# Layer 2 of a two-layer decoder trunk: weight splits of the gate's first units one step ahead, and the order of the splits at the start of the output projection

## The chip, the core and the metric

The kernel runs on one core of a Trainium2 chip. The metric is the device time of one execution in microseconds (us); lower is better. TensorE (PE in the profile, PEld for its weight loads) does the matrix products, VectorE (DVE) and ScalarE (ACT) do the elementwise work, GpSimd (POOL) takes a few small operations and issues the stores, and SyncE (SP) issues nearly all loads. Each engine takes its instructions strictly in the order in which the program lists them; between engines they wait for semaphores.

## The reference

Two layers of a decoder trunk, 512 tokens, width 2048, all in float32. The parts that matter here belong to layer 2, multi-head latent attention:

```
mod = (c_act @ ada_w[i] + ada_b[i])[:, None, :]
shift, scale, gate = jnp.split(mod, 3, axis=-1)
h = rmsnorm(x, norm_g[i]) * (1.0 + scale) + shift
...
proj = h @ w_in                      # cq, ckv, k_rope, g
...
o = causal_block_attention(q, k, v).reshape(B, S, MLA_WIDTH)
return (jax.nn.silu(g) * o) @ w_out
...
x = x + gate * y
```

After the two layers comes one final rmsnorm. Layer 1 has the same frame around a retention mixer; its output projection is the last product ahead of layer 2.

## The kernel before, in words

**Products.** Every float32 product is made of three passes. A weight tile and an activation tile are each split into a high part (rounded to the matmul's format) and a low part (the rest), and high x high, high x low and low x high are added up in PSUM (`mm3`, and the loops in `ga_half`, `o1_product`, `o2_product`). `split` (lines 134 to 136) makes the two parts: line 135 is a cast on ACT, line 136 a subtraction on DVE that needs the cast. A weight comes in units: a load on SP into one of three `raw` buffers, then a split into a pair of tiles. A raw buffer is free for the next load when the DVE half of its split has ended. Pairs come from three buffers in turn (`next_pair`), or, where a home is named, from another ring: `big` (16 buffers) or `k4b` (4 buffers).

**Steps.** Layer 1's projections, its output projection o1 and layer 2's input projections are a list of `Step`s. One loop walks it. For step i it issues the loads that are due, then `prepare_for(i + 1)`, which splits the weight units that the *next* step owns, then the step's own "form" work on DVE and ACT, then its matmuls. Loads run up to three units ahead of the splits. The names of the program are tiles: g2_0_u is unit u (256 rows) of the weights for the first 512 columns of layer 2's gate, `_r` its raw load and `_p` its parts.

**The end of layer 1.** The last four steps (`tail0` to `tail3`) finish o1 in halves of 256 tokens. Each finished block is scaled and added to the residual on DVE (`x1_out`, line 1430, giving x1), squared on ACT (line 1441), and the square is added up on DVE into x1_ss (line 1442).

**The norm ahead of layer 2.** For each half of the tokens, `norm_sums` lets PE add x1_ss over the partitions (line 1197); `token_factors` takes that sum through DVE (line 129, x_v in the profile), the reciprocal root on POOL (line 131), and two diagonal matrices on DVE (line 1204, x_diag); `norm_spread` lets PE spread the diagonals over all partitions (line 1212, x_r). `h2_pair` then forms two k-tiles of layer 2's input for one half: line 1580 (h2f, DVE), line 1587 (high part, ACT), line 1592 (low part, DVE).

**The front of layer 2.** Three steps, `front`, overlap the norm of the second token half with the gate's products on the first. `front0` multiplies unit 0 on half 0 (`ga_half`, line 1734), sums and roots half 1, forms k-tiles 4 and 5 on half 0, multiplies unit 1 on half 0 and spreads half 1's factors. Before the change unit 0 belongs to the last step of layer 1, unit 1 to `front[0]` and unit 2 to `front[1]`, so they are split during `tail2`, `tail3` and `front[0]`. `queued` and `behind` keep the written order on the engines named, against a scheduler that would otherwise move instructions by its own estimate.

**The start of the output projection o2.** After the last `attention_step` (heads 12 and 13, with the values v2_7 of heads 14 and 15), o2 runs in three rounds. Its first units interleave with heads 14 and 15: scores of 14, unit 0 of o2, scores of 15, unit 1, and so on. `o2_parts` loads two heads' results (o2_in) and splits them into o2_h and o2_l; `o2_unit` loads weights through `load_w` (raw tile o2_w0_u_raw) and splits them. The scheduler places the splits of units 1 and 2 among the attention's work, since only unit 0's input split is held in place by `queued`.

## Time and profile before

| what | us |
|---|---|
| median of three timed runs | 2124.95 (2124.93 to 2126.03) |
| the profiled execution's own time | 2125.97 |
| its span, first to last instruction | 2124.1 |
| PE busy | 2104.9 (99% of the span) |
| DVE busy | 1677.8 (79%) |
| ACT busy | 1056.4 (50%) |
| POOL busy | 106.2 (5%) |
| mean granted TensorE clock | 0.999 of full speed |

The span leaves 1.9 us of the profiled execution's time outside (2125.97 - 2124.1), and that execution is 1.0 us above the median. In the views, a row of the timeline gives start, duration, engine, source line, operation, output<-inputs and count; idle time ahead of it and what ended that follow in brackets. Matmuls overlap their successors, so a busy PE can hide short waits, and the pitch from start to start says more than the duration.

### The profile page before, as it was taken

To read this page: it belongs to the slowest core of one execution; us is meant where nothing else is said; L and a number is where in the kernel's file an instruction comes from. 1 tells how busy PE (TensorE), PEld (TensorE's weight loads), DVE (VectorE), ACT (ScalarE), POOL (GpSimd) and SP (SyncE) were. 2 spreads that over 40 slices of the span, in tenths; PEclk is the share of its full clock that TensorE was granted. 3 is DMA by queue.
4 is the path that set the end of the run, shared out by engine and by line. 5 is a ranking of instruction groups with operands and counts; after the bars stand their busy time and mean duration, and the time that the engine had idled before them with its cause. 6 is when DMAs were issued, how large, how long until landed. Compare 5 with 4: busy or idle time off the path is not lost.

```text
span 2124.1 us, 30010 instructions
## 1 busy us (share of the span) xinstructions
PE 2104.9 (99%) x11100; PEld 1811.2 (85%) x11100; DVE 1677.8 (79%) x2502; ACT 1056.4 (50%) x1622; POOL 106.2 (5%) x178
## 2 busy tenths in 40 slices
PE   8999999999999999999999999999999999999998
PEld 6878898989889888888888888898889989988887
DVE  7999788888888789666778777868978788886655
ACT  6764444444454444434344544445446575664434
POOL 1000010000000000000000000010001000000000
PEclk9999999999999999999999999999999999999999
DMA  9976787868787778755647565853466634346644
GB/s 380 406 282 199 232 276 226 276 216 269 241 262 248 245 228 281 266 170 197 232 157 251 184 222 209 276 177 112 160 189 208 194 123 149 121 133 225 217 137 141
DMA packets 229957, 462.95 MB, mean 218 GB/s; under 512 B 20865, under 2 KB 84385, under 8 KB 226097
## 3 DMA queue, kind: packets, MB, share of 16 engines
q1 hardware_dynamic: 217600, 421.85, 60.2%
q0 software_dynamic: 11920, 38.91, 4.7%
q8 instruction: 87, 1.43, 0.3%
q14 instruction: 60, 0.49, 0.1%
q10 hardware_dynamic: 290, 0.27, 0.0%
HBM read 417.96 MB, written 43.00 MB: 217 GB/s over the span
## 4 chain that ended last, share of the span: by engine, by line
PE 94%; DVE 2%; DMA 2%; issue 1%; ACT 1%; POOL 0%; SPq 0%; POOLq 0%; DVEq 0%; ACTq 0%
PE o L1464 16%; PE o L2418 4%; PE x L873 2%; PE x L874 2%; PE y L874 2%; PE y L873 2%; PE s L874 2%; PE s L873 2%; PE x L875 2%; PE y L875 2%; PE s L875 2%; PE s_qk L974 2%; PE x_qk L974 2%; PE y_qk L974 2%; PE qk L158 2%; PE qk L160 2%
## 5 line engine op out<-in xcount | busy, mean ns | idle before, releaser
L1464 PE MATMUL o<-o_h,o_p 128*128 128x512 f32 (+1 forms) x1088 | 323.1, 378 | 0.0
L1464 PEld LDWEIGHTS o<-o_h,o_p 128*128 128x128 f32 x1088 | 200.1, 188 | 37.2
L1464 PE MATMUL o<-o_l,o_p 128*128 128x512 f32 (+1 forms) x544 | 204.8, 376 | 0.0
L1464 PEld LDWEIGHTS o<-o_l,o_p 128*128 128x128 f32 x544 | 102.3, 188 | 18.4
L136 DVE TENSOR_TENSOR o_p<-o_r,o_p 128x1024 fp32r<-128x1024 f32 x64 | 78.2, 1223 | 38.0 <-ACT o_p L135 37.0
L1160 DVE SCALAR_TENSOR_TENSOR mod<-mod,c_odd 128x1024 f32<-128x1024 f32 x56 | 67.8, 1221 | 23.3 <-DMA mod<-in_ada_t_dram 23.3
L2418 PE MATMUL o<-o_h,o_w 128*128 128x512 f32 (+1 forms) x320 | 82.1, 346 | 0.0
L135 ACT CAST o_p<-o_r 128x1024 fp32r<-128x1024 f32 x64 | 66.6, 1052 | 24.4 <-PE o L1464 17.2
L158 PE MATMUL qk<-hT,qk_p 128*128 128x512 f32 x192 | 75.1, 391 | 0.1
L159 PE MATMUL qk<-hT,qk_p 128*128 128x512 f32 x192 | 74.7, 389 | 0.0
L160 PE MATMUL qk<-hT,qk_p 128*128 128x512 f32 x192 | 74.4, 390 | 0.0
L389 DVE SCALAR_TENSOR_TENSOR aw<-aw,c_all 128x2048 f32<-128x2048 f32 (+1 forms) x36 | 73.2, 2049 | 0.7 <-DMA aw<-in_ada_t_dram 0.7
L2418 PEld LDWEIGHTS o<-o_h,o_w 128*128 128x128 f32 x320 | 55.9, 188 | 7.5
L136 DVE TENSOR_TENSOR o_l<-o_in,o_h 128x1024 fp32r<-128x1024 f32 x24 | 29.3, 1223 | 39.0 <-ACT o_h L135 39.0
L135 ACT CAST o_h<-o_in 128x1024 fp32r<-128x1024 f32 x24 | 25.3, 1054 | 62.6 <-PE o L159 44.7
L2418 PE MATMUL o<-o_l,o_w 128*128 128x512 f32 (+1 forms) x160 | 55.2, 345 | 0.0
L1319 ACT ACTIVATE yn<-y,nmr,gn_r 128x512 f32<-128x512 f32 x32 | 22.3, 778 | 62.3 <-DVE nmr L1313 62.3
L159 PE MATMUL o<-o_l,o_w 128*128 128x512 f32 x128 | 49.9, 390 | 0.6 <-DVE o_l L136 0.6
L158 PE MATMUL o<-o_h,o_w 128*128 128x512 f32 x128 | 50.1, 391 | 0.0
L160 PE MATMUL o<-o_h,o_w 128*128 128x512 f32 x128 | 49.8, 389 | 0.0
L136 DVE TENSOR_TENSOR o_w<-o_w_raw,o_w 128x1024 fp32r<-128x1024 f32 x32 | 38.9, 1220 | 12.8 <-ACT o_w L135 12.8
L1160 DVE SCALAR_TENSOR_TENSOR mod<-mod,c_bm 128x1024 f32<-128x1024 f32 x40 | 48.7, 1218 | 0.0
(1532 smaller groups left out, 6246.3 us busy)
## 6 DMA issues: line engine op xcount, KB each, us to landing
mod<-in_ada_t_dram SPq DMA_DIRECT2D x96, 512.0 KB, 5.6
o_r<-in_ret_w_out_dram SPq DMA_DIRECT2D x64, 512.0 KB, 5.6
aw<-in_ada_t_dram SPq DMA_DIRECT2D x29, 1024.0 KB, 9.5
mod_gate<-in_ada_t_dram SPq DMA_DIRECT2D x32, 512.0 KB, 4.4
o_w_raw<-in_mla_w_out_dram SPq DMA_DIRECT2D x32, 512.0 KB, 4.7
qk_r<-in_ret_w_in_dram SPq DMA_DIRECT2D x48, 256.0 KB, 3.1
qk_r<-qk_d SPq DMA_DIRECT2D x32, 256.0 KB, 5.7
v_r<-v_d SPq DMA_DIRECT2D x32, 256.0 KB, 6.6
```

Source lines behind the costliest of these rows:

```text
L135: ACT.copy(hi, src)
L136: DVE.tensor_sub(lo, src, hi.bitcast(F32))
L158: PE.matmul(o, lhs[0], rhs[0], start=first and not seeded, stop=False, skip_group_check=seeded)
L159: PE.matmul(o, lhs[0], rhs[1], start=False, stop=False, skip_group_check=seeded)
L160: return PE.matmul(o, lhs[1], rhs[0], start=False, stop=last, skip_group_check=seeded)
L873: PE.matmul(banks[b], a[0], w[0], start=first, stop=False, skip_group_check=True)
L874: PE.matmul(banks[b], a[0], w[1], start=False, stop=False, skip_group_check=True)
L875: PE.matmul(banks[b], a[1], w[0], start=False, stop=True, skip_group_check=True)
L974: PE.matmul(o, w[wp][:, i, b * P : (b + 1) * P], a[ap], start=first and i + b + k == 0, stop=k == 2, skip_group_check=True,)
L1160: DVE.scalar_tensor_tensor(out=aw, in0=aw, scalar=1.0, in1=silu_c[j], op0=ALU.mult, op1=ALU.mult, accum_out=row_sums[piece][:, j, b : b + 1],)
L1464: PE.matmul(o, w[i][:, ki, c0 + b * P : c0 + (b + 1) * P], a[j], start=first and i + j == 0, stop=last and i == 1, skip_group_check=True,)
L2418: PE.matmul(banks2[b][:, cols], w[0][i][:, 0, b * P : (b + 1) * P], o2_moving(w, u, cols)[j], start=u + i + j == 0, stop=u == KD - 1 and i ...
```

## The change

Three things are changed, all in the order of work; no arithmetic is added or removed.

1. The gate's units 0, 1 and 2 are owned by the steps one earlier each (`steps[-2]`, `steps[-1]`, `front[0]`), so they are split in `tail1`, `tail2` and `tail3`. Unit 2's parts get two `k4b` buffers as their home and no longer take a pair, so that units 3 and later use the pairs in another turn.
2. In `front0`, the first halves of k-tiles 4 and 5 (h2f, and the high parts) are issued between the reciprocal root and the diagonals of half 1.
3. At the start of o2, the loads and splits of weight units 1 and 2 are held behind the ACT and the DVE half of the first input's split (`o2_first`), and head 14's score work on DVE is held behind that split too.

```
--- before.py
+++ after.py
@@ -804,7 +804,7 @@
             self.rows, self.sums = rows, sums
             self.beside = {"load": [], "early": [], "form": [], "multiply": []}
 
-    def plain_steps(nu, kn, parts, cn, name, take, n, lhs, rhs, evac, seeded=False, halved=0, **kw):
+    def plain_steps(nu, kn, parts, cn, name, take, n, lhs, rhs, evac, seeded=False, halved=0, homes={}, **kw):
 
         banks = {}
 
@@ -817,7 +817,7 @@
                     nc.sync.dma_start(dst(w["raw"]), src)
 
             def prepare():
-                w["hl"] = two_tiles(None, [P, kn, cn], f"{name}_{u}_p", ASIDE if u < halved else EVEN)
+                w["hl"] = two_tiles(homes.get(u), [P, kn, cn], f"{name}_{u}_p", ASIDE if u < halved else EVEN)
                 split(w["raw"], *w["hl"])
 
             def multiply():
@@ -1196,9 +1196,10 @@
         for t in range(n0, n0 + n):
             PE.matmul(ps[:, t : t + 1], ss[:, t * P : (t + 1) * P], crow, start=True, stop=True)
 
-    def token_factors(ps, n0, n, name):
+    def token_factors(ps, n0, n, name, between=lambda: None):
 
         r = rsqrt(ps[:, n0 : n0 + n], n, 1.0 / D, name)
+        between()
         diag = tmp(f"{name}_diag")
         for t in range(n):
             DVE.tensor_scalar(
@@ -1561,8 +1562,8 @@
             norm2["s"] = aux("x1_sums")
         token_sums(norm2["s"], ss1[0], 2 * half, 2)
 
-    def norm_factors(half):
-        norm2["diag"] = token_factors(norm2["s"], 2 * half, 2, f"x1_{half}")
+    def norm_factors(half, between=lambda: None):
+        norm2["diag"] = token_factors(norm2["s"], 2 * half, 2, f"x1_{half}", between)
 
     def norm_spread(half):
 
@@ -1717,7 +1718,7 @@
         )
 
 
-    ga = g2_steps(0, seeded=True, halved=3)
+    ga = g2_steps(0, seeded=True, halved=3, homes={2: 2 * (("k4b", 4),)})
 
     def ga_half(u, th):
 
@@ -1778,16 +1779,16 @@
     def front0():
         ga_half(0, 0)
         norm_sums(1)
-        queued(norm_factors, 1)
-        queued(h2_pairs, (2, 0))
+        lows = []
+        queued(norm_factors, 1, lambda: lows.append(queued(h2_pair, 2, 0)))
+        queued(lows[0])
         ga_half(1, 0)
         norm_spread(1)
         queued(h2_pairs, (0, 1), (1, 1), (2, 1))
 
     front = [Step() for _ in range(3)]
-    steps[-1].units = ga[0].units
-    front[0].units = ga[1].units
-    front[1].units = ga[2].units
+    for step, unit_step in zip((*steps[-2:], front[0]), ga):
+        step.units = unit_step.units
     front[0].multiply = front0
     front[1].multiply = lambda: (ga_half(2, 0), ga_half(0, 1), queued(h2_pairs, (3, 0), (3, 1), (4, 0)))
     front[2].multiply = lambda: (ga_half(1, 1), ga_half(2, 1), queued(h2_pairs, (4, 1), (5, 0), (5, 1)))
@@ -2362,11 +2363,18 @@
         return hi, lo
 
     o2_split = {(0, 0): queued(o2_parts, 0, 0)}
-    scored(last[0])
+    o2_first = [next(i for i in reversed(nc.cur_bb.bb.instructions) if i.engine == e) for e in (A_, V_)]
+    with behind(V_):
+        scored(last[0])
 
     def o2_unit(r, u, kn, cn, where=None):
         halved = kn == 1 and u >= KD - 4
-        wt = load_w([(whole, rows(w_mla_out, u, kn, r * T, cn))], kn, cn, f"o2_w{r}_{u}", where=where, halved=halved)
+        with ExitStack() as stack:
+            for ins in o2_first if (r, u) in ((0, 1), (0, 2)) else ():
+                stack.enter_context(tc.issue_after(ins))
+            wt = load_w(
+                [(whole, rows(w_mla_out, u, kn, r * T, cn))], kn, cn, f"o2_w{r}_{u}", where=where, halved=halved
+            )
         k = r, u * kn // 2
         if k not in o2_split:
             o2_split[k] = o2_parts(*k)
```

**First place: DVE at the end of layer 1 and in `front0`.** x1_ss is the sum of squares, x1_1_v the first step of half 1's root, h2f_0_4 and h2f_0_5 k-tiles 4 and 5 on half 0. Before:

```order
L1442 TENSOR_TENSOR x1_ss_11899<-x1_ss_11899,x1_sq0_3_1_12548 128x256
L136 TENSOR_TENSOR g2_0_2_p_12563<-g2_0_2_r_12245,g2_0_2_p_12563 128x1024
L129 TENSOR_SCALAR x1_1_v_12596<-x1_sums_12394 128x2
L1204 TENSOR_SCALAR x1_1_diag_12600<-ident_70,x1_1_r_12598 128x128 x2
L1580 SCALAR_TENSOR_TENSOR h2f_0_4_12603<-x1_2_8934,a_col1_91,x1_r0_12433 128x256
L1580 SCALAR_TENSOR_TENSOR h2f_0_5_12607<-x1_2_8934,a_col1_91,x1_r0_12433 128x256
L1592 SCALAR_TENSOR_TENSOR h2_4_12605<-h2f_0_4_12603,b_col1_92,h2_4_12605 128x256
L1592 SCALAR_TENSOR_TENSOR h2_5_12609<-h2f_0_5_12607,b_col1_92,h2_5_12609 128x256
```

The same place in the changed kernel (the source lines shift by one):

```order
L1443 TENSOR_TENSOR x1_ss_11899<-x1_ss_11899,x1_sq0_3_1_12554 128x256
L129 TENSOR_SCALAR x1_1_v_12599<-x1_sums_12399 128x2
L1581 SCALAR_TENSOR_TENSOR h2f_0_4_12603<-x1_2_8934,a_col1_91,x1_r0_12438 128x256
L1581 SCALAR_TENSOR_TENSOR h2f_0_5_12607<-x1_2_8934,a_col1_91,x1_r0_12438 128x256
L1205 TENSOR_SCALAR x1_1_diag_12611<-ident_70,x1_1_r_12601 128x128 x2
L1593 SCALAR_TENSOR_TENSOR h2_4_12605<-h2f_0_4_12603,b_col1_92,h2_4_12605 128x256
L1593 SCALAR_TENSOR_TENSOR h2_5_12609<-h2f_0_5_12607,b_col1_92,h2_5_12609 128x256
```

The split of unit 2 (g2_0_2) has left the space between the last sum and x1_1_v, and the two h2f rows have moved ahead of the diagonals. Splits of units 0, 1 and 2 now stand where nothing, unit 0 and unit 1 stood.

**Second place: ACT at the start of o2.** v2_7 are the values of heads 14 and 15, o2_h0_0 the high part of o2's first input, p_14 the probabilities of head 14. Before:

```order
L1918 CAST v2_7_0_17719<-uv_7_0_17686 128x2x256
L135 CAST o2_w0_1_17916<-o2_w0_1_raw_17914 128x1024
L1918 CAST v2_7_1_17744<-uv_7_1_17693 128x2x256
L135 CAST o2_w0_2_17973<-o2_w0_2_raw_17971 128x1024
L135 CAST o2_h0_0_17774<-o2_in0_17772 128x1024
L2068 ACTIVATE p_14_0_17787,sm_14_17786<-a_14_0_17780,nb_14_0_17792 128x128
L135 CAST o2_h0_1_17921<-o2_in1_17919 128x1024
```

Changed:

```order
L1919 CAST v2_7_0_17720<-uv_7_0_17687 128x2x256
L1919 CAST v2_7_1_17745<-uv_7_1_17694 128x2x256
L135 CAST o2_h0_0_17775<-o2_in0_17773 128x1024
L135 CAST o2_w0_1_17917<-o2_w0_1_raw_17915 128x1024
L135 CAST o2_h0_1_17922<-o2_in1_17920 128x1024
L135 CAST o2_w0_2_17974<-o2_w0_2_raw_17972 128x1024
L2069 ACTIVATE p_14_0_17788,sm_14_17787<-a_14_0_17781,nb_14_0_17793 128x128
```

The first input's cast went ahead of both weight casts. On DVE, the same place, before (o2_13 is head 13's gated result, nb_14 the row maxima of head 14):

```order
L136 TENSOR_TENSOR o2_w0_1_17916<-o2_w0_1_raw_17914,o2_w0_1_17916 128x1024
L1180 TENSOR_TENSOR gate_c1_93<-mod_1_2_0_s_17741,vcol_84 128x8
L1919 TENSOR_TENSOR v2_7_1_17744<-uv_7_1_17693,v2_7_1_17744 128x2x256
L2113 TENSOR_TENSOR o2_13_17760<-o_13_17747,sg2_13_17424 128x512
L136 TENSOR_TENSOR o2_w0_2_17973<-o2_w0_2_raw_17971,o2_w0_2_17973 128x1024
L2065 TENSOR_TENSOR a_14_0_17780<-a_14_0_17780,mask_75 128x128
L2065 TENSOR_TENSOR a_14_1_17795<-a_14_1_17795,mask_75 128x128
L2067 TENSOR_REDUCE nb_14_0_17792<-a_14_0_17780 128x1
L136 TENSOR_TENSOR o2_l0_0_17775<-o2_in0_17772,o2_h0_0_17774 128x1024
L2067 TENSOR_REDUCE nb_14_1_17802<-a_14_1_17795 128x1
```

Changed:

```order
L1920 TENSOR_TENSOR v2_7_1_17745<-uv_7_1_17694,v2_7_1_17745 128x2x256
L2114 TENSOR_TENSOR o2_13_17761<-o_13_17748,sg2_13_17425 128x512
L136 TENSOR_TENSOR o2_l0_0_17776<-o2_in0_17773,o2_h0_0_17775 128x1024
L2066 TENSOR_TENSOR a_14_0_17781<-a_14_0_17781,mask_75 128x128
L2066 TENSOR_TENSOR a_14_1_17796<-a_14_1_17796,mask_75 128x128
L2068 TENSOR_REDUCE nb_14_0_17793<-a_14_0_17781 128x1
L2066 TENSOR_TENSOR a_14_2_17806<-a_14_2_17806,mask_75 128x128
L2066 TENSOR_TENSOR a_14_3_17816<-a_14_3_17816,mask_75 128x128
L136 TENSOR_TENSOR o2_w0_1_17917<-o2_w0_1_raw_17915,o2_w0_1_17917 128x1024
L2068 TENSOR_REDUCE nb_14_1_17803<-a_14_1_17796 128x1
```

The low part of the first input, o2_l0_0, now stands ahead of both weight splits; unit 1's split comes after head 14's four masks, and unit 2's (not shown) after the reciprocal of head 14's sums.

**Third place: SP's queue at the start of o2.** o2_w0_4 and o2_w0_5 take the raw buffers of units 1 and 2. Before:

```order
L2358 DMA o2_in3_18049<-o2_d_68 128x2x512
L142 DMA o2_w0_4_raw_18095<-in_mla_w_out_dram 128x2x512
L2358 DMA o2_in4_18100<-o2_d_68 128x2x512
L2128 DMA c_gate10_18130<-c_d_69 128x1024
L2134 DMA mod_gate_100_18132<-in_ada_t_dram 128x1024
L142 DMA o2_w0_5_raw_18134<-in_mla_w_out_dram 128x2x512
```

Changed:

```order
L2359 DMA o2_in3_18050<-o2_d_68 128x2x512
L2359 DMA o2_in4_18101<-o2_d_68 128x2x512
L2129 DMA c_gate10_18131<-c_d_69 128x1024
L142 DMA o2_w0_4_raw_18096<-in_mla_w_out_dram 128x2x512
L2135 DMA mod_gate_100_18133<-in_ada_t_dram 128x1024
L142 DMA o2_w0_5_raw_18135<-in_mla_w_out_dram 128x2x512
```

Unit 4's load went behind the load of o2_in4 and the gate's row of c; the rest keeps its order.

34 lines of the change are left out of this document (21 added, 13 removed).

## The prediction

> **What bounds the kernel now.** I read the page's sums first, then, in the second fence, the rows of PE's list of waits that lie at the change (us in total, times, longest).
>
> ```profile
> PE 2104.9 (99%) x11100; PEld 1811.2 (85%) x11100; DVE 1677.8 (79%) x2502; ACT 1056.4 (50%) x1622; POOL 106.2 (5%) x178
> ```
>
> ```profile
> PE x_r L1212 <- DVE x_diag L1204: 0.7, 1, 0.7
> PE o L159 <- DVE o_l L136: 0.6, 1, 0.6
> PE g L1734 <- ACT h L1587: 0.4, 1, 0.4
> ```
>
> PE is busy for 99% of the span, and the change takes no matmul away. It can only win back waits of PE, and these three are all that lie where it edits: 1.7 us. So the question is whether they go, what they cost beyond their own length, and whether others come. A difference of 0.2% (4.25 us) is about what a measurement of this kernel can tell from no change, and 1.7 us is below that.
>
> The first and third wait are one place, the front of layer 2. The timeline from 1430.9 us (start, duration, engine, line, operation, tiles, count, idle before):
>
> ```profile
> 1430.89 0.50 PE L1197 MATMUL x_sums<-ones,x_ss 128*128 128x1 f32 x4
> 1431.17 1.23 DVE L136 TENSOR_TENSOR g_p<-g_r,g_p 128x1024 fp32r<-128x1024 f32 x1 [0.51 <-ACT g_p L135]
> 1431.26 1.89 PE L1734 MATMUL g<-h,g_p 128*128 128x256 f32 x14
> 1432.31 0.15 DVE L129 TENSOR_SCALAR x_v<-x_sums 128x2 f32<-128x2 f32 x1
> 1432.62 0.72 POOL L131 TENSOR_TENSOR x_r<-x_v,few 128x2 f32<-128x2 f32 x1 [2.09 <-DVE x_v L129]
> 1433.37 0.48 DVE L1204 TENSOR_SCALAR x_diag<-ident,x_r 128x128 f32<-128x128 f32 x2 [0.91 <-POOL x_r L131]
> 1433.77 0.87 DVE L1580 SCALAR_TENSOR_TENSOR h2f<-x,a_col,x_r 128x256 f32<-128x256 f32 x2
> 1433.80 0.68 PE L1212 MATMUL x_r<-x_diag,ones 128*128 128x128 f32 x4 [0.65 <-DVE x_diag L1204]
> 1434.28 0.91 ACT L1587 ACTIVATE h<-h2f,b_col 128x256 fp32r<-128x256 f32 x2 [3.14 <-DVE h2f L1580]
> 1434.84 11.63 PE L1734 MATMUL g<-h,g_p 128*128 128x256 f32 x96 [0.35 <-ACT h L1587]
> ```
>
> PE's sum is there at 1431.39 (1430.89 + 0.50), but x_v starts at 1432.31: DVE is in the split of gate unit 2 (g_p), which had itself waited for its cast. From x_v on there is one chain, x_v, POOL, diagonals, PE; only then h2f, ACT, PE. Half 0 of the same norm ran without such a split in front:
>
> ```profile
> 1418.07 0.61 PE L1197 MATMUL x_sums<-ones,x_ss 128*128 128x1 f32 x4
> 1418.71 0.16 DVE L129 TENSOR_SCALAR x_v<-x_sums 128x2 f32<-128x2 f32 x1 [0.70 <-PE x_sums L1197]
> 1420.40 0.28 PE L1464 MATMUL o<-o_l,o_p 128*128 128x256 f32 x1
> 1420.73 0.68 PE L1212 MATMUL x_r<-x_diag,ones 128*128 128x128 f32 x4
> 1421.17 0.48 PE L1464 MATMUL o<-o_h,o_p 128*128 128x256 f32 x2
> ```
>
> It shows the two prices without a wait: x_v starts 0.03 us behind the sum (1418.71 against 1418.68), and the spread of the factors starts 0.05 us behind the end of the matmul before it (1420.73 against 1420.68), with the next product 0.44 us after the spread's start.
>
> The second wait is at the start of o2:
>
> ```profile
> 1920.85 1.05 ACT L135 CAST o_h<-o_in 128x1024 fp32r<-128x1024 f32 x1
> 1922.09 1.22 DVE L136 TENSOR_TENSOR o_w<-o_w_raw,o_w 128x1024 fp32r<-128x1024 f32 x1
> 1923.81 1.22 DVE L136 TENSOR_TENSOR o_l<-o_in,o_h 128x1024 fp32r<-128x1024 f32 x1
> 1924.07 0.40 PE L158 MATMUL o<-o_h,o_w 128*128 128x512 f32 x1
> 1925.08 0.49 PE L159 MATMUL o<-o_l,o_w 128*128 128x512 f32 x1 [0.62 <-DVE o_l L136]
> 1925.42 0.39 PE L160 MATMUL o<-o_h,o_w 128*128 128x512 f32 x1
> 1925.64 0.40 PE L158 MATMUL o<-o_h,o_w 128*128 128x512 f32 x1
> ```
>
> PE's first matmul of o2 runs at 1924.07; the second needs the low part o_l, which DVE starts at 1923.81, behind a weight split (o_w) that PE needs only a unit later.
>
> **The change, part by part.**
>
> *Unit 2's split leaves the gap ahead of x_v.* DVE then waits for the sum alone: x_v at 1431.39 + 0.03 = 1431.42, 0.89 us earlier. POOL followed x_v by 0.31 us and took 0.72, the diagonals followed POOL's end by 0.03: diagonals at 1432.48. *h2f goes ahead of them*: it fills DVE from 1431.57 to 1432.44 (0.87), about as long as POOL takes, so it delays the diagonals by nothing. The spread ran 0.43 us after the diagonals' start (1433.37 to 1433.80), so its data would be ready at 1432.91. PE comes from its 14 products at 1431.26 + 1.89 = 1433.15, and starts 0.05 us later, as in half 0: 1433.20. That is **0.60 us** saved, with 0.29 us in hand.
>
> *Unit 1's turn to unit 2.* The product after the spread started 1.04 us behind the spread's start (1433.80 to 1434.84), against 0.44 us in half 0. It waited for ACT's high part. That now follows h2f by 0.51 us as before (1433.77 to 1434.28): it starts at 1432.08 and both are done by 1433.0, ahead of the product at 1433.20 + 0.44 = 1433.64. Saved: 1.04 - 0.44 = **0.60 us**. What is late next is the low part (line 1592), now the third item behind x_v: DVE ends the diagonals at 1432.96 and the first low part by about 1433.4, an estimate from half of the two-tile durations here; PE wants it a matmul after 1433.64. The listed order now takes all three passes of a block in turn; that costs nothing as long as this holds, and up to about 0.3 us otherwise.
>
> *The splits that move to tail1 and tail2.* Units 0, 1 and 2 take the DVE and ACT places that nothing, unit 0 and unit 1 had, so only unit 0's place is new, on DVE and ACT behind the squares of tail0:
>
> ```profile
> 1409.27 0.42 ACT L1441 ACTIVATE x_sq<-x 128x256 f32<-128x256 f32 x1 [1.00 <-DVE x L1430]
> 1410.17 0.48 DVE L1430 SCALAR_TENSOR_TENSOR x<-o,gate_c,o_xr 128x256 f32<-128x256 f32 x1
> 1415.46 0.43 DVE L1442 TENSOR_TENSOR x_ss<-x_ss,x_sq 128x256 f32<-128x256 f32 x1 [0.55 <-ACT x_sq L1441]
> ```
>
> The loads of units 0 and 1 were issued at the two ends of this row:
>
> ```profile
> L817 SPq DMA_DIRECT2D g_r<-in_mla_w_in_dram x2: 378/378/379, 1396.5 to 1398.2; - x2
> ```
>
> ACT is free at 1409.69, casts for 1.03, DVE subtracts for 1.23 until about 1412.0; the residual step of 1410.17 slips 1.8 us, and the next three follow as fast as DVE goes. The last sum of that step needs the last square, whose PE block has not moved, so it still ends near 1415.9; PE uses it at 1418.07. Cover: 2.2 us, cost nothing. Even with the longest landing quoted below, 9.5 us, the second is there at 1407.7. The loads of units 3 to 5 start up to 8 us earlier; PE waits for none of them now.
>
> *Unit 2 in `k4b`.* The trace has no gate unit there. The pitch of 96 products in pairs is (11.63 - 0.28) / 95 = 0.119 us with a little waiting in it. Layer 1's tail runs on a mix of homes (two units in `big`, one in `k4b`, one in a pair):
>
> ```profile
> L1464 PE MATMUL o<-o_l,o_p x40: 276/283/283, 1403.0 to 1416.8; 128*128 128x256 f32 x40
> ```
>
> One of three products is listed: 13.8 / (39 x 3) = 0.118 us. So I take zero for 48 products, with 0.25 us either way, from the 0.113 to 0.119 that such products show (durations of 0.276 to 0.283).
>
> *The start of o2.* On ACT two weight casts fewer stand ahead of o_h, so it ends at its old 1921.90 at the latest. On DVE the low part takes the place that unit 2's weight split had, 1922.09, at the latest, since unit 1's has left too: it ends by 1923.3. PE wants it one pitch after 1924.07, at 1924.30. The second matmul then starts 0.23 us behind the first and not 1.01: 0.78 saved; the third 0.23 and not 0.34 behind the second (1925.42 to 1925.64 is the usual 0.22 to 0.23): 0.11. Together **0.89 us**, with 1 us in hand. What is queued behind the new holds: head 14's masks, its maxima and so ACT's exponentials and head 15's scores, which need the PSUM of head 14's. By the list those end within about 3 us after 1924.2, and PE reaches head 15's scores only after 24 products of 0.227, at 1929.5. Unit 1's weights, split by about 1925.6, are wanted after those scores.
>
> *Loads behind the later splits.* Units 4 and 5 reuse the raw buffers of units 1 and 2. Their issues and their casts:
>
> ```profile
> 1920.92 0.37 SPq L142 DMA_DIRECT2D o_w_raw<-in_mla_w_out_dram  x1
> 1923.33 0.72 SPq L142 DMA_DIRECT2D o_w_raw<-in_mla_w_out_dram  x1
> 1941.22 1.08 ACT L135 CAST o_w<-o_w_raw 128x1024 fp32r<-128x1024 f32 x1
> 1946.60 1.04 ACT L135 CAST o_w<-o_w_raw 128x1024 fp32r<-128x1024 f32 x1
> ```
>
> The slowest 512 KB loads between 1900 and 1930 (issues, size, median us to landing):
>
> ```profile
> mod_gate<-in_ada_t_dram SPq DMA_DIRECT2D x2, 512.0 KB, 9.5
> ```
>
> The two loads slip to about 1925.6 and 1929.3, and the gate's rows and o_in behind them on SP as well. Even at 9.5 us they land by 1935.1 and 1938.8; their casts come at 1941.22 and 1946.60 less the 2.1 us saved. Cover 4 us and more: cost nothing.
>
> **Sum.** 0.60 + 0.60 + 0.89 = 2.09 us, all of it waits of PE, and PE's list shows no other wait between these places and the end's. The profiled execution would go from 2125.97 to 2123.9, the median of 2124.95 to **2122.9**.
>
> **Rivals.**
>
> 1. *POOL is held up by h2f.* In the new order POOL's root runs beside h2f. The trace has both outcomes for a root beside DVE work:
>
> ```profile
> 16.53 1.66 POOL L131 TENSOR_TENSOR x_r<-x_v,few 128x1 f32<-128x1 f32 x1 [0.52 <-DVE x_v L129]
> 16.55 1.22 DVE L389 SCALAR_TENSOR_TENSOR aw<-aw,c_all 128x1024 f32<-128x1024 f32 x1
> 2112.99 0.68 DVE L2473 TENSOR_TENSOR y<-x,x_r 128x512 f32<-128x512 f32 x1
> 2113.15 0.70 POOL L131 TENSOR_TENSOR x_r<-x_v,few 128x2 f32<-128x2 f32 x1 [5.65 <-DVE x_v L129]
> ```
>
> At 16.53, beside an operation on two SBUF tiles, the root took 1.66 us and ended 0.42 after DVE; at 2113.15, beside one with its second input in PSUM, it took the usual 0.70. h2f is of the second kind (x1 in SBUF, the spread in PSUM), so I expect no delay. If it were held, POOL would end 0.42 to 0.72 after 1432.44, the diagonals start at 1432.9 to 1433.2 and the spread at 1433.3 to 1433.6 in place of 1433.20: 0.1 to 0.4 us given back, 2123.0 to 2123.3. The Trainium skill, in "SBUF — State Buffer", section "Who interferes with whom", states both: a DVE instruction with two SBUF inputs shuts out a GpSimd instruction that reads SBUF, and one with at most one SBUF input, outside the two-port modes, does not. Both rows agree with it, and by it the sum stays at 2.09 us.
> 2. *One place gains, the other not*, since the low part in front or the first input's split in o2 is late by an order that I misread: only 0.89 or 1.20 saved, 2124.1 or 2123.8.
> 3. *No change.* The waits go, but PE arrives 2 us early at data that come at their own time (DMA), or the scheduler's holds put a wait of the same size elsewhere: 2125.0. Against it: from 1435 to 1924 PE waits for nothing named.
> 4. *Slower: the late loads of o2.* Units 4 and 5, issued 4.7 and 6.0 us later on an SP queue with the gate's rows behind them, come too late. It decides from a landing of unit 4 after 1939.1 or unit 5 after 1944.5, some 13.5 to 15 us after issue; each microsecond beyond is one on PE, and above 2.1 us the kernel is slower than before. At 5 us late: 2127.9. The longest landing seen (9.5) speaks against it.
>
> **Chances.** Forecast 0.72, rival 1 0.09, rival 2 0.08, rival 3 0.06, rival 4 0.05. The range takes the forecast with 0.6 us for the unknown prices and 0.5 us for the spread of the runs (2124.93 to 2126.03) below, and rivals 1 and 2 above: 2121.8 to 2124.4. Faster by over 0.2% would be under 2120.7, which no case reaches: 0.02. Slower by over 0.2% is over 2129.2, the far end of rival 4: 0.03. The rest, 0.95, is within 0.2%.
>
> **What would show it.** Right: PE's list of waits has lost all three rows; x_v starts about 0.03 us after the sum; the spread follows the 14 products without idle time; line 159 follows line 158 at o2's start by 0.23 us. Wrong: a new row in PE's list for line 1734 on the low parts (line 1592), for line 1464 or the sums in the tail, or for o2 on a weight split; a root on POOL well over 0.72 us; o2 casts that wait for DMA.

## The result and the profile after

The changed kernel takes 2123.40 us (median of 22 runs, 2122.35 to 2124.24), the kernel before 2126.24 us (22 runs, 2124.93 to 2127.44; two of its first three runs, from which the prediction started, are the fastest of all). The ratio is 0.9987 with a 95% interval of 0.9981 to 0.9993: faster by 0.13%. Forecast was a gain of 2.09 us; by the medians it is 2.84, by the spans of the two profiled executions 2124.1 - 2121.3 = 2.8. The direction and the places were right, and the gain is about a third larger than forecast. The forecast time of 2122.9 us lies only 0.5 us under the measured 2123.40 because two errors cancel, which is luck: the level it started from, 2124.95, was 1.29 us under the median of 22 runs, and the gain was 0.75 us too small. The prediction also held 0.2% (4.25 us) to be about what can be told from no change; with 22 runs of each kernel, 2.84 us could be.

The sums of the page after:

```profile
span 2121.3 us, 30012 instructions
PE 2103.4 (99%) x11100; PEld 1811.2 (85%) x11100; DVE 1677.6 (79%) x2502; ACT 1055.0 (50%) x1622; POOL 105.9 (5%) x178
```

PE's busy time is 1.5 us less for the same 11100 matmuls, a first hint that more than named waits has gone. PE's whole list of waits after (us in total, times, longest):

```profile
PE c_ps L471 <- DMA c_all<-in_c_dram: 3.1, 1, 3.1
PE xT_ps L471 <- DVE x_diag L564: 2.6, 3, 1.6
PE qk L445 <- ACT hT L417: 1.7, 2, 1.2
PE v L445 <- ACT hT L417: 0.8, 1, 0.8
PE x_sums L2457 <- DVE x_ss L2404: 0.5, 1, 0.5
PE x_sums L2457 <- ACT x_sq L2399: 0.2, 1, 0.2
```

All that is left lies at the kernel's start and end. The three rows of before (x_r, g and o, 1.7 us) are gone and no row has come. The front of layer 2 in the timeline of the changed kernel, one engine after another (start, duration, engine, line):

```profile
1430.89 0.50 PE L1197 MATMUL x_sums<-ones,x_ss 128*128 128x1 f32 x4
1431.25 1.90 PE L1735 MATMUL g<-h,g_p 128*128 128x256 f32 x14
1432.98 0.62 PE L1213 MATMUL x_r<-x_diag,ones 128*128 128x128 f32 x4
1433.36 11.43 PE L1735 MATMUL g<-h,g_p 128*128 128x256 f32 x96
...
1431.42 0.16 DVE L129 TENSOR_SCALAR x_v<-x_sums 128x2 f32<-128x2 f32 x1 [0.78 <-PE x_sums L1197]
1431.50 0.86 DVE L1581 SCALAR_TENSOR_TENSOR h2f<-x,a_col,x_r 128x256 f32<-128x256 f32 x2
1432.48 0.48 DVE L1205 TENSOR_SCALAR x_diag<-ident,x_r 128x128 f32<-128x128 f32 x2
1432.88 0.88 DVE L1593 SCALAR_TENSOR_TENSOR h<-h2f,b_col,h 128x256 fp32r<-128x256 f32 x2
...
1431.73 0.71 POOL L131 TENSOR_TENSOR x_r<-x_v,few 128x2 f32<-128x2 f32 x1 [1.23 <-DVE x_v L129]
...
1432.01 0.91 ACT L1588 ACTIVATE h<-h2f,b_col 128x256 fp32r<-128x256 f32 x2 [1.82 <-DVE h2f L1581]
```

x_v at 1431.42 and the diagonals at 1432.48 are where the prediction put them, to 0.01 us. But PE runs the spread at 1432.98, not at 1433.20, and the product behind it at 1433.36, not at 1433.64. The start of o2:

```profile
1918.04 1.05 ACT L135 CAST o_h<-o_in 128x1024 fp32r<-128x1024 f32 x1
1919.91 1.22 DVE L136 TENSOR_TENSOR o_l<-o_in,o_h 128x1024 fp32r<-128x1024 f32 x1
1922.35 0.39 PE L158 MATMUL o<-o_h,o_w 128*128 128x512 f32 x1
1922.58 0.39 PE L159 MATMUL o<-o_l,o_w 128*128 128x512 f32 x1
1922.81 0.39 PE L160 MATMUL o<-o_h,o_w 128*128 128x512 f32 x1
```

o_l is done at 1921.13, and the second and third matmuls follow by 0.23 us each.

How the gain adds up, with both kernels' times counted from the start of the gate's first product (1427.04 before, 1427.03 after), so that what wanders ahead of it doesn't count:

| place | before | after | gain | forecast |
|---|---|---|---|---|
| spread of half 1's factors starts | 6.77 | 5.95 | 0.82 | 0.60 |
| the product behind it starts, from the spread's start | 1.04 | 0.38 | 0.66 | 0.60 |
| 96 products, first start to the next 512-column one | 11.46 | 11.26 | 0.20 | 0 |
| o2, first matmul to the 25th | 6.38 | 5.44 | 0.94 | 0.89 |

That is 2.62 of the 2.85 us between the two spans. Of the rest, 0.04 us lies between the two places and 0.2 behind o2's last matmul, where no instruction was changed; its cause stays open. Equal code differs by more than that from run to run (the gate's first product came between 1426.02 and 1427.44 in the kernels below). So each experiment is read by its times from the gate's first product on, and by its median only beside that.

### The profile page after: what moved, and what is told of

It is laid out like the page before. It is cut to its first block, busy times and chain, and to the rows that moved or that the text cites. A ratio compares the mean times of both kernels' runs of the same rounds, so it can differ in the third digit from the quotient of the medians.

```text
span 2121.3 us, 30012 instructions
## 1 busy us (share of the span) xinstructions
PE 2103.4 (99%) x11100; PEld 1811.2 (85%) x11100; DVE 1677.6 (79%) x2502; ACT 1055.0 (50%) x1622; POOL 105.9 (5%) x178
## 4 chain that ended last, share of the span: by engine, by line
PE 94%; DMA 2%; DVE 1%; issue 1%; ACT 1%; POOL 0%; SPq 0%; DVEq 0%; POOLq 0%; ACTq 0%
PE o L1465 15%; PE o L2426 4%; PE x L874 2%; PE x L873 2%; PE y L874 2%; PE s L874 2%; PE y L873 2%; PE s L873 2%; PE x L875 2%; PE s L875 2%; PE y L875 2%; PE uv L2028 2%; PE s_qk L974 2%; PE x_qk L974 2%; PE y_qk L974 2%; PE qk L158 2%
```

## The experiments

Each run gives the same marks: spread, next product and first 512-column product of the gate, counted from the gate's first product, and in o2 the steps from the first to the second and from the second to the third matmul. T is the time from the first 256-column product of layer 1's tail to the gate's first. A product here is one matmul. Each ratio is to runs of the kernel before that were taken along with that kernel, with a 95% interval.

| kernel | T | spread | next | 512 columns | o2 steps | median us (runs), ratio to before |
|---|---|---|---|---|---|---|
| before | 24.17 | 6.77 | 7.80 | 19.26 | 1.02, 0.33 | 2126.24 (22) |
| changed | 24.20 | 5.95 | 6.33 | 17.59 | 0.23, 0.23 | 2123.40 (22), 0.9987 [0.9981, 0.9993] |
| e1_front | 24.20 | 5.95 | 6.33 | 17.59 | 1.02, 0.34 | 2124.23 (11), 0.9993 [0.9984, 1.0002] |
| e2_o2 | 24.17 | 6.75 | 7.78 | 18.84 | 0.23, 0.23 | 2124.43 (11), 0.9994 [0.9985, 1.0003] |
| e3_steps | 24.21 | 5.95 | 6.92 | 18.49 | 1.02, 0.34 | 2124.87 (10), 0.9995 [0.9986, 1.0004] |
| e4_between | 24.17 | 6.75 | 7.19 | 18.58 | 1.02, 0.34 | 2125.34 (10), 0.9996 [0.9987, 1.0006] |
| e5_even | 24.42 | 5.95 | 6.32 | 17.59 | 0.23, 0.23 | one run, 2123.3 |
| e6_residual | 23.90 | 6.12 | 6.48 | 17.75 | 0.23, 0.23 | 2123.49 (10), 0.9987 [0.9978, 0.9997] |
| e7_pool | 24.20 | 6.21 | 6.65 | 17.92 | 0.23, 0.23 | one run, 2123.45 |
| e8_scores | 24.21 | 5.95 | 6.32 | 17.59 | 0.42, 0.33 | one run, 2123.04 |
| e9_weights | 24.19 | 5.95 | 6.33 | 17.61 | 0.24, 0.23 | one run, 2123.27 |
| e10_tail | 23.59 | 6.12 | 6.49 | 17.77 | 0.23, 0.23 | 2123.03 (11), 0.9987 [0.9978, 0.9995] |
| e12_reset | 24.17 | 6.75 | 7.79 | 19.12 | 1.01, 0.34 | one run, 2125.26 |
| e13_best | 23.59 | 6.07 | 6.44 | 17.71 | 0.23, 0.23 | 2122.78 (11), 0.9984 [0.9975, 0.9993] |

The marks repeat to 0.02 us wherever the code is the same, but for the third, which the products' pitch moves (below); the medians of ten runs don't separate kernels that differ by under a microsecond.

### One part at a time: e1_front and e2_o2

e1_front undoes the o2 part of the changed kernel, e2_o2 undoes the front:

```diff
-    with behind(V_):
-        scored(last[0])
+    scored(last[0])
...
-            for ins in o2_first if (r, u) in ((0, 1), (0, 2)) else ():
+            for ins in o2_first if False else ():
```

> The front part alone (steps moved, k4b home, h2f ahead of the diagonals); the start of o2 is as before the change. Theory: the front is worth what the changed kernel's trace shows there, PE 1.64 us earlier at the end of the gate's 256-column products (0.82 at the spread, 0.66 at the product behind it, 0.17 to 0.20 by a shorter pitch of the products behind), and the wait of 0.6 us at o2 is back: about 1.6 us under the kernel before, span near 2122.4. Rival: only the 1.20 us of the prediction come from here, and the rest of the 2.8 us is wander of the runs: span near 2122.9, and PE 1.20 us earlier behind the spread's products.

Measured: all marks of the front are those of the changed kernel, 19.26 - 17.59 = 1.67 us ahead of before; o2 waits again. So the 1.6 us and not 1.20 belong to the front. By the medians it is 1.9 us (2124.23 against 2126.1 for the kernel before, taken along with it).

> The o2 part alone (holds on weights 1 and 2 and on head 14's score work); the front is as before the change. Theory: 0.89 us under the kernel before (0.78 at the second matmul of o2, 0.11 at the third), o_l at once behind the cast o_h, PE's list without a row at line 159, and the waits of 0.7 and 0.4 us at the spread and at the gate still there. Rival: PE reaches o2 later than with both parts, so the data have 1.6 us more and the holds do nothing that a smaller edit would not; then the gain is the same 0.89. Against the theory would be a gain under 0.5 us or a new wait behind head 15's scores.

Measured: o2's two steps are 0.23 us, as in the changed kernel, and the front's two waits are back (6.75 and 7.78). The parts are separate. By the medians e2_o2 is 1.7 us under the kernel before (2124.43 against 2126.1), where 0.89 were expected. What was not expected is the third mark, 18.84 against 19.26, with the same front as before; that is taken up below.

### The two halves of the front: e3_steps and e4_between

e3_steps is e1_front with h2f behind the diagonals again:

```diff
-        lows = []
-        queued(norm_factors, 1, lambda: lows.append(queued(h2_pair, 2, 0)))
-        queued(lows[0])
+        queued(norm_factors, 1)
+        queued(h2_pairs, (2, 0))
```

> Steps moved and k4b home, but h2f stays behind the diagonals; o2 as before. Theory (two separate waits): the diagonals keep their new time and the spread is still 0.82 us earlier, but h2f starts 0.40 us behind the diagonals' start, ACT 0.91 and the product 1.47 us behind it, so the product starts 0.97 us behind the spread and not 0.38: 0.59 us of the front are given back, about 1.0 us left. Rival (one chain: once the split is gone everything moves up together): the product starts 0.38 us behind the spread as well, and all 1.6 us stay.

The timeline of e3_steps:

```profile
1433.40 0.62 PE L1213 MATMUL x_r<-x_diag,ones 128*128 128x128 f32 x4
1434.37 11.73 PE L1735 MATMUL g<-h,g_p 128*128 128x256 f32 x96 [0.35 <-ACT h L1588]
```

e4_between is e1_front with the splits in their old steps and unit 2 in a pair:

```diff
-    for step, unit_step in zip((*steps[-2:], front[0]), ga):
-        step.units = unit_step.units
+    steps[-1].units = ga[0].units
+    front[0].units = ga[1].units
+    front[1].units = ga[2].units
...
-    ga = g2_steps(0, seeded=True, halved=3, homes={2: 2 * (("k4b", 4),)})
+    ga = g2_steps(0, seeded=True, halved=3)
```

> h2f ahead of the diagonals, but the splits stay in their old steps and unit 2 in a pair; o2 as before. Theory: x_v still waits for unit 2's split, the spread starts as in the kernel before (0 gained), h2f then runs beside the root, ACT's high part is done by the spread, and the product starts about 0.38 us behind the spread and not 1.04: 0.66 us gained. By the first theory and this one the two halves of the front add up (0.82 + 0.66, and the pitch). Rival: without the moved split DVE is so late that h2f delays the diagonals, and the spread is up to 0.5 us later: 0.1 to 0.2 us gained in all.

The timeline of e4_between:

```profile
1433.39 0.68 PE L1213 MATMUL x_r<-x_diag,ones 128*128 128x128 f32 x4 [0.64 <-DVE x_diag L1205]
1433.83 11.55 PE L1735 MATMUL g<-h,g_p 128*128 128x256 f32 x96
```

At the spread and at the product behind it both theories hold. With the steps moved alone the spread has no wait and the product has (0.97 us behind the spread); with h2f moved alone it is the other way round (0.44 behind). The gains at the product, 0.88 and 0.61 us, add up to 1.49, and the two together gave 1.47: two waits one behind the other, each with its own cause.

What the theories miss lies behind that product. e3_steps was expected to keep about 1.0 us and keeps 0.77 (19.26 - 18.49). Its first three steps behind the spread take 0.22, 0.30 and 0.22 us, e1_front's 0.20, 0.12 and 0.12: the third matmul waits for DVE's low part, which begins at 1434.35 there and ends at 1434.83, and starts at 1434.89. So in the moved steps h2f's new place is worth 0.90 us, 0.59 by the high part and 0.31 by the low part behind it.

### Why the spread gained 0.82 and not 0.60: e6_residual

The prediction took the price of a spread without a wait from half 0, where it starts 0.33 us behind the start of the product before it. In the changed kernel half 1's spread starts 0.12 us behind the last product's start (1432.98 against 1432.87), a plain pitch. In the changed kernel's half 0, an instruction of PE that waits for DVE's semaphore runs at 1420.61, just ahead of the spread at 1420.72, and DVE ends the residual step of block (1, 1), which is queued behind the diagonals there, at 1420.58. That step empties the PSUM bank into which the spread goes. Half 0 in the changed kernel, the residual step, the product before the spread, and the spread:

```profile
1420.10 0.48 DVE L1431 SCALAR_TENSOR_TENSOR x<-o,gate_c,o_xr 128x256 f32<-128x256 f32 x1
1420.38 0.28 PE L1465 MATMUL o<-o_l,o_p 128*128 128x256 f32 x1
1420.72 0.68 PE L1213 MATMUL x_r<-x_diag,ones 128*128 128x128 f32 x4
```

e6_residual puts the residual step between root and diagonals:

```diff
-        norm_sums(0)
-        queued(norm_factors, 0)
-        tail_block(1, 1, 1)
-        queued(out_behind, 1, 1, 1)
+        norm_sums(0)
+        tail_block(1, 1, 1)
+        queued(norm_factors, 0, lambda: queued(out_behind, 1, 1, 1))
         tail_block(1, 2, 1)
-        norm_spread(0)
         queued(out_behind, 1, 2, 1)
+        tail_block(1, 3, 1, (4, 5, 6))
+        queued(norm_spread, 0)
         lows = queued(h2_pair, 0, 0)
-        tail_block(1, 3, 1)
+        tail_block(1, 3, 1, (7,))
```

> The changed kernel, and in half 0 of the norm the residual step of block (1, 1) goes between the root and the diagonals, as h2f does in half 1; the spread is kept two products ahead of its old place. Theory (the 0.33 us in which half 0's spread follows the product before it hold a wait of 0.22 us for the PSUM bank that this residual step frees, so that the prediction's price of a spread was 0.22 too high): the spread follows the product before it by 0.11 to 0.12 us, as in half 1 of the changed kernel, and the gate's first product is 0.22 us earlier. Rival (0.33 is what a switch from these products to the spread costs): the pitch stays 0.33, and nothing is won.

The spread of half 0 in its timeline, and the product ahead of it:

```profile
1420.76 0.28 PE L1465 MATMUL o<-o_h,o_p 128*128 128x256 f32 x1
1420.88 0.60 PE L1213 MATMUL x_r<-x_diag,ones 128*128 128x128 f32 x4
```

0.12 us, so the 0.33 held a wait of 0.21 that no list of waits names: all but 0.06 of it lies under the modelled end of the product before (1420.66), and those 0.06 stand as "issue" in the profile's chain. T falls by 0.30, since the start behind a gap is late as well (the spread's second matmul follows by 0.11 us here, by 0.18 behind the gap). At the front 0.16 us are given back. The scheduler now puts half 1's sums behind 29 products and not 34, but e13_best below shows that the place of the sums is only about a third of it; the rest is the products' pitch. By the marks 0.14 us are left of the 0.30, and by the median the kernel is where it was (2123.49).

### What h2f beside the root costs: e7_pool

```diff
+        if half == 0:
+            norm2["copy"] = l1_tile("yn", 4, "x1_r_copy")[:, :H]
+            ACT.copy(norm2["copy"], norm2["r", 0][:, :H])
...
-                in1=norm2["r", half][:, cols],
+                in1=norm2["copy"] if (u, half) == (2, 0) else norm2["r", half][:, cols],
```

> The changed kernel, but the h2f that runs beside the root of half 1 reads the spread from a copy in SBUF (one more copy on ACT in the tail), so that both its inputs are in SBUF. Theory (rival 1 of the prediction was averted by the input in PSUM): the root is now held up, 1.1 to 1.7 us and not 0.71, the diagonals come 0.3 to 0.9 us later, and the spread 0.1 to 0.6 later than 5.95 us behind the gate's first product. Rival (such an operation does not hold POOL up at this place): the root keeps 0.71 and the spread 5.95.

POOL and DVE in its timeline:

```profile
1431.97 0.82 POOL L131 TENSOR_TENSOR x_r<-x_v,few 128x2 f32<-128x2 f32 x1 [1.14 <-DVE x_v L129]
1431.74 0.87 DVE L1584 SCALAR_TENSOR_TENSOR h2f<-x,a_col,x_r_copy 128x256 f32<-128x256 f32 x2
1432.83 0.48 DVE L1205 TENSOR_SCALAR x_diag<-ident,x_r 128x128 f32<-128x128 f32 x2 [0.22 <-POOL x_r L131]
```

Neither theory has the number. The root is held, but by 0.11 us and not by 0.4 to 1.0: the two halves of h2f are 0.47 us each, and the root ends 0.18 us behind the second. The diagonals start 1.17 us behind x_v and not 1.06. (The sums come 0.20 us later here, presumably a cost of the copy on ACT, so 6.21 is not the price of the root.) The Trainium skill, "SBUF — State Buffer", section "Who interferes with whom", has a DVE instruction with two SBUF inputs contend with GpSimd's reads, and one with a single SBUF input not: the runs agree in both cases, with 0.82 and 0.71 us, but at this place the difference is only 0.11 us (one run with both inputs in SBUF; the same root beside h2f took 0.71 to 0.72 us in the changed kernel, e1_front, e5_even and e8_scores).

### Are both holds in o2 needed: e8_scores and e9_weights

e8_scores drops the hold on the weights (the second hunk of e1_front's diff), e9_weights the one on head 14's score work (the first hunk).

> The changed kernel without the holds on weight units 1 and 2 of o2; only head 14's score work stays held behind the first input's split. Theory (the low part comes from behind two things, a weight split and the masks, and one of the two out of the way would do): the casts of both weight units are ahead of o_h again, o_h ends near 1920.1 and o_l near 1922.2, and PE's second matmul of o2, wanted near 1922.6, still follows the first by 0.23 us; head 14's score work is 1.2 us later, which may cost up to 0.5 us before head 15's scores. Rival (both holds are needed, as the change has them): the second matmul waits again, by 0.3 to 0.6 us.

The start of o2 in the timeline of e8_scores:

```profile
1921.20 1.22 DVE L136 TENSOR_TENSOR o_l<-o_in,o_h 128x1024 fp32r<-128x1024 f32 x1
1922.05 0.40 PE L158 MATMUL o<-o_h,o_w 128*128 128x512 f32 x1
1922.47 0.49 PE L159 MATMUL o<-o_l,o_w 128*128 128x512 f32 x1
```

> The changed kernel without the hold on head 14's score work; weight units 1 and 2 stay held behind the first input's split. Theory (as for the kernel with the other hold alone): o_h ends near 1919.1 as in the changed kernel, o_l comes behind two masks and two maxima on DVE, from about 1921.2 to 1922.4, and the second matmul of o2 still follows the first by 0.23 us, with 0.1 us in hand. Rival: both holds are needed, and the second matmul waits 0.3 to 0.6 us.

The same in e9_weights:

```profile
1921.35 1.22 DVE L136 TENSOR_TENSOR o_l<-o_in,o_h 128x1024 fp32r<-128x1024 f32 x1
1922.51 0.40 PE L158 MATMUL o<-o_h,o_w 128*128 128x512 f32 x1
1922.75 0.39 PE L159 MATMUL o<-o_l,o_w 128*128 128x512 f32 x1
```

The theory that either would do was half right. Without the weights' hold o_l comes 0.19 us too late for the second matmul, and 0.34 of the 0.94 us are lost over the first 24; the expected cost before head 15's scores did not come. With the weights' hold alone nothing measurable is lost (5.46 against 5.44 for the first 24), with o_l ready 0.18 us ahead of its use. Alone, the hold on the score work saves 0.60 of the 0.94 us; beside the weights' hold it brings margin and no time.

### The products' pitch: e5_even and e12_reset

The same 256-column products run at three pitches, and the duration of a row gives them away: 276 ns goes with a pitch of 0.113 us, 279 with 0.118, 283 with 0.120. The rows of the gate's line over the 96 products behind the spread (ns min/median/max, first and last start), before and e2_o2, whose front is the same code:

```profile
L1734 PE MATMUL g<-h,g_p x89: 279/279/280, 1435.6 to 1445.9; 128*128 128x256 f32 x89
```

```profile
L1735 PE MATMUL g<-h,g_p x88: 276/276/276, 1435.4 to 1445.3; 128*128 128x256 f32 x88
```

(1445.9 - 1435.6) / 88 = 0.117 and (1445.3 - 1435.4) / 87 = 0.114: over 96 products this is the 0.42 us by which e2_o2's third mark differs. In the changed kernel the middle 48 (units 0 and 1 on half 1) and the last 24 (unit 2):

```profile
L1735 PE MATMUL g<-h,g_p x47: 276/276/283, 1436.2 to 1441.4; 128*128 128x256 f32 x47
L1735 PE MATMUL g<-h,g_p x22: 278/283/283, 1441.6 to 1444.1; 128*128 128x256 f32 x22
```

I matched the trace's matmuls to the SBUF addresses in the built program. All gate activations begin in the upper half of a block of 128 bytes. The pairs of units 0 and 1 begin in the lower half, the k4b buffers in the upper. (Half here means 64 bytes.) Over the whole changed kernel, 667 steps between 256-column products with both operands in the same half have a median of 120 ns, 2374 with operands in different halves one of 113 ns. e5_even puts unit 2 into a pair again, 64 bytes further on, and the tail's last unit into k4b:

```diff
-            {4: 2 * (("big", 16),), 5: 2 * (("big", 16),), 6: 2 * (("k4b", 4),)}.get(u),
+            {4: 2 * (("big", 16),), 5: 2 * (("big", 16),), 6: 2 * (("k4b", 4),), 7: 2 * (("k4b", 4),)}.get(u),
...
-    ga = g2_steps(0, seeded=True, halved=3, homes={2: 2 * (("k4b", 4),)})
+    ga = g2_steps(0, seeded=True, halved=2)
```

> The changed kernel with unit 2's parts in a pair again (as before the change) but 64 bytes further on in it, at the offset that units 3 to 7 have; the last unit of layer 1's tail takes the k4b buffers in its place. Theory (64 bytes): a product of 256 columns takes 0.113 us where weights and activations begin in different halves of 128 bytes, and 0.120 where in the same half, whatever the ring is called; so unit 2 keeps 0.120 in the pair, the tail's last unit goes from 0.113 to 0.120, and the rest of the gate's products has 0.113 or 0.118. Rival (the ring): k4b is slow and a pair is fast; unit 2 then runs at 0.113 to 0.118. The waits at the front stay as in the changed kernel (spread 5.95 us behind the gate's first product, next product 6.33).

Unit 2 on half 0 in e5_even:

```profile
L1735 PE MATMUL g<-h,g_p x19: 280/283/284, 1434.1 to 1436.2; 128*128 128x256 f32 x19
```

Unit 2 keeps 283 ns in the pair, and the tail's last unit, now in k4b, goes from 0.113 to 0.120 (T is 0.22 longer). It is the 64 bytes, not the ring. That it is the relation of the two operands, and not the place of the weights alone, shows in the changed kernel: 288 of the 2374 steps have the activations in the lower half and the weights in the upper, where unit 2's are, and take 113 ns as well.

e12_reset moves unit 2 by the 64 bytes alone, in the kernel before:

```diff
-    ga = g2_steps(0, seeded=True, halved=3)
+    ga = g2_steps(0, seeded=True, halved=2)
```

> The kernel before with one edit: unit 2's parts lie 64 bytes further on in their pair. Theory (products at 0.118 are a state that a gap leaves behind where weights and activations lie in different halves of 128 bytes, and a run of products in the same half ends it): unit 2's 24 products on half 0 take 0.120 each, the 48 behind them (units 0 and 1 on half 1) 0.113, unit 2's second 24 again 0.120. Rival (the state ends or stays by chance, as two kernels with the same front had 0.118 and 0.113): the 48 take 0.118 as before.

Unit 2 on half 0, then units 0 and 1 on half 1, in e12_reset:

```profile
L1734 PE MATMUL g<-h,g_p x14: 280/283/283, 1435.5 to 1437.1; 128*128 128x256 f32 x14
L1734 PE MATMUL g<-h,g_p x47: 276/276/283, 1437.3 to 1442.6; 128*128 128x256 f32 x47
```

The run at 0.120 is followed by 0.113, with the waits and code of the kernel before. By itself that leaves the rival open: e2_o2 left the state at a step of 169 ns close behind the spread, with no run at 0.120, and e12_reset has such a step too. The cleaner pair is e1_front and e4_between: the first step behind the spread is alike (202 and 201 ns), and the 48 products have 0.113 in e1_front, behind a run at 0.120, and 0.118 in e4_between, without one. In all 11 kernels of the table with unit 2 in the same half as the activations the 48 have 0.113; in the three without (before, e4_between, e2_o2) the state stayed twice and was left once. So the runs support that a run at 0.120 ends the state, with one trace for each kernel.

### Further along the same line: e10_tail and e13_best

e10_tail frees both PSUM banks of half 0 early; beside the edits of e6_residual (with the spread behind the second unit of the block):

```diff
-                split(w["raw"], *w["hl"])
+                if (name, u) == ("g2_0", 1):
+                    ACT.copy(w["hl"][0], w["raw"])
+                    late_low.append(
+                        lambda: DVE.tensor_sub(w["hl"][1], w["raw"], w["hl"][0].bitcast(F32))
+                    )
+                else:
+                    split(w["raw"], *w["hl"])
...
         queued(out_behind, 1, 0, 1)
-        norm_sums(0)
...
+        queued(late_low.pop())
         tail_block(1, 1, 1)
+        queued(norm_sums, 0)
```

> The changed kernel, and in half 0 the residual step of block (1, 0) ahead of the low part of unit 1's split, the sums behind block (1, 1), the residual step of block (1, 1) between root and diagonals, and the spread behind the second unit of block (1, 3). Theory (both waits of half 0 are for PSUM banks that a residual step frees late): the sums follow the product before them by 0.11 and not 0.32 us, the spread by 0.12 and not 0.33: 0.42 us less from the tail's start to the gate's first product, 0.4 us under the changed kernel, near 2123.0. Rival (as for the kernel with the residual step alone): nothing is won, or the split that is moved behind the residual step delays x_v by up to 0.3 us and the spread waits for the diagonals.

Measured: T is 0.61 us shorter (more than 0.42, since behind the gaps the second matmul was late too: by 0.18 and not 0.11 us in the spread, by 0.13 and not 0.03 in the sums), and 0.18 are given back at the front: 0.43 us in all. That this is the 0.42 expected is luck: 0.19 more were won and 0.18 lost. e13_best is e10_tail with half 1's sums held where the changed kernel has them:

```diff
         ga_half(0, 0)
-        norm_sums(1)
+        ga_half(1, 0, slice(0, 3))
+        queued(norm_sums, 1)
...
-        ga_half(1, 0)
+        ga_half(1, 0, slice(3, 8))
```

> The kernel with the residual steps of half 0 in the waits, and half 1's sums put back to where the changed kernel has them (behind 33 products of the gate and not 26). Theory: the spread comes 5.95 us behind the gate's first product again and not 6.12, the end of the 256-column products 17.6 behind it and not 17.77, and from the tail's start on the kernel is 0.55 to 0.6 us faster than the changed one: span near 2120.8, time near 2122.9. Rival: the 0.17 us come from the state of the products (0.118 for 0.113) and not from the place of the sums; then 6.12 stays.

Measured: the spread comes at 6.07, the 512-column products at 17.71. A third of the 0.17 us was the place of the sums; the rest is pitch, the rival's case: behind a step of 0.146 us between the gate's 13th and 14th product, 33 ns over the others, the products take 0.118 up to the sums. What makes that step late stays open. From the tail's first 256-column product to the gate's first 512-column one e13_best takes 41.30 us, the changed kernel 41.79, before 43.43: 0.49 us less than the changed kernel, where 0.55 to 0.6 were expected. Its median of 2122.78 (2122.28 to 2123.45) is the lowest of all; that it beats the changed kernel by 0.5 us rests on one trace of each, while the two ranges of times overlap.

## Why the prediction was right, and where its sizes were off

- **Bound and place.** Nearly all of the gain is waits of PE (2.42 of the 2.62 us that the marks show), and the three rows went from the list without a new one. Right.
- **x_v, h2f, root, diagonals.** x_v starts 0.03 us behind the sum, the diagonals start at 1432.48 with h2f ahead of them, and the root takes 0.71 us. Right to 0.01 us. Rival 1 did not occur, and its price was too high: it let POOL end 0.42 us or more behind h2f, and with both inputs in SBUF (e7_pool) POOL ended 0.18 behind.
- **"PE comes from its 14 products at 1431.26 + 1.89 = 1433.15, and starts 0.05 us later, as in half 0": the term that was mis-sized, 0.60 for a measured 0.82.** A matmul starts a pitch behind the last one's start (0.12 us), not behind its modelled end, and half 0, which was to show the price without a wait, held a hidden wait of 0.21 (e6_residual). For the same reason the time in hand was not 0.29 us but about 0.07: by the prediction's own step from the diagonals the data are there at 1432.91, and PE takes them at 1432.98.
- **The product behind the spread**: measured 0.66 for 0.60. Half 0's 0.44 us from the spread to the next product held part of the same delay, and 0.38 is the price. The first low part ends near 1433.36 (0.48 us from 1432.88), ahead of the second matmul behind the spread at 1433.56. In e3_steps it is late and costs the 0.3 us that the prediction named.
- **Unit 0's split in `tail1`**: forecast a slip of the residual step of 1.8 us and no cost. The changed kernel's timeline of DVE:

```profile
1410.61 1.23 DVE L136 TENSOR_TENSOR g_p<-g_r,g_p 128x1024 fp32r<-128x1024 f32 x1 [0.51 <-ACT g_p L135]
1411.76 0.87 DVE L1431 SCALAR_TENSOR_TENSOR x<-o,gate_c,o_xr 128x256 f32<-128x256 f32 x2
1415.45 0.42 DVE L1443 TENSOR_TENSOR x_ss<-x_ss,x_sq 128x256 f32<-128x256 f32 x1 [0.55 <-ACT x_sq L1442]
```

  The residual step of 1410.17 now starts at 1411.76, a slip of 1.6 us, and the last sum is at its old place. T differs by 0.03 us. Right.
- **Unit 2 in `k4b`: zero, with 0.25 us either way.** Its own 48 products take 0.120 us, the longest pitch of the three. (The 0.118 that the prediction took from the tail is a mean that hides this: by address, three of the tail's four units have both operands in the same half and run at 0.120, the one in k4b among them, and the one in a pair at 0.113.) But the 48 products between them fall from 0.118 to 0.113, and with slightly shorter first steps behind the spread the 96 products take 0.20 us less. Inside the bound, but the sign is luck: against the state that e2_o2 found (18.84 - 7.78 = 11.06 us for these products) the changed kernel's 11.26 lose 0.20.
- **o2**: measured 0.79 and 0.10 us for 0.78 and 0.11, and 0.05 more over the next twenty matmuls. Right. The prediction did not see that the weights' hold alone gives the cover on DVE (e9_weights).
- **Late loads**: forecast to land with 4 us to spare. Their issues, and the casts that use them:

```profile
1924.00 0.37 SPq L142 DMA_DIRECT2D o_w_raw<-in_mla_w_out_dram  x1
1927.77 0.37 SPq L142 DMA_DIRECT2D o_w_raw<-in_mla_w_out_dram  x1
1938.58 1.08 ACT L135 CAST o_w<-o_w_raw 128x1024 fp32r<-128x1024 f32 x1
1943.94 1.05 ACT L135 CAST o_w<-o_w_raw 128x1024 fp32r<-128x1024 f32 x1
```

  14.6 and 16.2 us lie between them, and the loads of this tile took at most 4.4. Rival 4 did not occur. The 9.5 us that the prediction calls the longest landing are the median of two loads; the longer took 10.3, which would still have left 3.2 us.

So the sum 0.60 + 0.60 + 0.89 became 0.82 + 0.66 + 0.94, and 0.20 of pitch. The first two differences are explained by e6_residual and the marks; how often the kernel before leaves the state of 0.118 by itself stays open, and with it how much of the 0.20 the change owns.

## What to carry to other kernels

Work that stands ahead of a short chain through several engines can cost PE most of its length (here 0.82 us for a split of 1.23), and the gap in which one engine computes a root is the place to put work of another; find the instruction at the head of each wait, since two waits in a row may have two causes and then two repairs that add up. Take the price of a step "without a wait" from starts, not from modelled ends, and only from a place where nothing was late: a wait for a PSUM bank can lie under a modelled end and show as a little "issue" (0.21 us in half 0, of which 0.06 showed). Hold back what stands ahead of the needed operand (the weights), and test whether a second hold does anything beside the first.

## What the runs showed of the hardware

- A 256-column product takes 0.113 us when weights and activations begin in different halves of 128 bytes, 0.120 when in the same half (medians of 2374 and 667 steps of one trace; e12_reset moves one unit's weights by 64 bytes alone, and its products go from 0.118 to 0.120). Products of 512 columns with both in the same half take 0.227 us (median of 7140 steps), twice 0.113, which suggests that it costs nothing there; all 512-column products of that trace have both in the same half, so the two cases were not compared. The Trainium skill, "TensorE: Matmul & The Clock Gate", section "Step-by-step: what each phase is for", says that loading the next tile's weights does not take read bandwidth from the running matmul; here the 512-column products give no sign against that, while 6.7 ns of each 256-column one depend on where the weights lie. Whether it is the load of the weights that costs them, no run shows.
- Where the halves differ, the products can run at 0.118 us for dozens of them behind a gap (of 33 ns already, in e13_best). A gap can also end that (e2_o2), and behind a run at 0.120 it was always over (11 kernels). What makes the state was not tried.
- Without a wait, a switch of operand kinds costs little: a spread follows a product by 0.12 us, and the next product follows the spread's four matmuls 0.38 us behind their start.
